# Position-biased softmax on one core: the first chunk in one transfer, a bias table of 16 packets, and a last cut of two rows on eleven and nine DMA engines

## The chip, the cores and the metric

The kernel runs on one core of one Trainium2 chip. The metric is device microseconds for one execution. Before the change the median of three runs is 1329.23 us (1328.12 to 1330.56). One more execution was taken under the hardware profiler; all rows of a profile come from that execution.

## The reference

The inputs are `logits` of shape (2, 8, 2112, 2112) and `rel_bias` of shape (8, 33), both float32. The bias depends only on the head and on the distance between row and column, clipped to 16 on either side.

```python
rel = pos[:, None] - pos[None, :]
bias = rel_bias[:, np.clip(rel, -16, 16) + 16]
logits = logits + bias[None, :, :, :]
logits = logits - logits.max(axis=-1, keepdims=True)
exp = np.exp(logits)
return (exp / exp.sum(axis=-1, keepdims=True)).astype(np.float32)
```

So 285.5 MB of logits come in, and as much goes out.

## The kernel before

**Tiling.** The 2 x 8 x 2112 rows of 2112 numbers are dealt out in order: each of the 128 partitions owns 264 consecutive rows (`ROWS`), an eighth of one head. A chunk is six rows (`R`) of every partition, 128 x 12672 numbers, 6336 KB, and there are 44 chunks. Four buffers X0 to X3 hold chunks; a chunk is loaded into its buffer, worked on in place, and stored from there.

**The table.** VectorE first builds a strip M of 2375 numbers per partition in PSUM, from which the bias of any row is a window. For that, L101 loads all 264 numbers of `rel_bias` to each of the 128 partitions (on ScalarE's DMA queue), L135 multiplies by a mask that leaves the partition's own head, L139 adds over the eight heads into `rbS`, and L143 to L159 spread the result into M. The iotas of L105 and L106 on GpSimd tell each partition its head and its eighth.

**The steady loop.** For every four chunks VectorE copies a window of M to F (L164). Per chunk it then does six fused passes that add the bias, negate, and take the minimum, which is minus the row's maximum (L170); ScalarE does six exponentials with a sum (L179); VectorE takes three reciprocals at a time (L187) and scales the rows (L191).

**The DMA queue.** All loads and stores of logits are issued by SyncE (SP), in the order of the program. First stand the loads of chunk 0, as six transfers of one row per partition (L92; the first five count up the semaphore `pre`, the sixth counts up `ld[0]`), and the loads of chunks 1 to 3 (L82). VectorE waits for `pre` ahead of its loop (L194). In SP's loop (L208) a store waits until its rows are scaled (L85), and the load of chunk n + 4 waits until the store of chunk n has landed (L211), as they share a buffer.

**The end.** The last chunk is stored in four transfers: rows 0 to 2 of it on 128 partitions (L215), and then the list `TAIL` (L217): the rest up to column `CUT` of the chunk's 12672 on 128 partitions, then the columns from `CUT` on, for partitions 0 to 109, and the same columns for partitions 110 to 127. Here `CUT` is 12672 - 768, so the last two transfers hold 768 numbers (3072 bytes) of each partition. The list is laid out for a split of each transfer over the core's 16 DMA engines by partitions: eight partitions to each engine out of 128, ten to each of eleven engines out of 110 (`MOST` is written as 11 * 10), and two to each of nine engines out of 18. SP's final waits (L226, L227) end the program.

Of the kernel before, what the change touches and what calls it, by code (L numbers as in the profile page):

```python
# [15 lines left out]
def kernel(  # L16
# [6 lines left out]
    nc = tc.nc  # L23
    P = 128
    B, H, S, S2 = logits.shape
    assert S == S2
    MR = 16
    W = 2 * MR + 1
    ROWS = B * H * S // P
    PB = S // ROWS  # L30
    assert ROWS * P == B * H * S and PB * ROWS == S and PB == H == 8
    R = 6
    NBUF = 4
# [4 lines left out]
    MW = S + ROWS - 1  # L38
    FW = S + STEP - 1
    BIG = 3.0e38  # L40
    CUT = R * S - 768
    MOST = 11 * 10
    TAIL = [(0, P, HALF * S, CUT), (0, MOST, CUT, R * S), (MOST, P, CUT, R * S)]

    io = ctx.enter_context(tc.tile_pool(name="io", bufs=1))
    X = [io.tile([P, R * S], FP32, tag=f"X{b}", name=f"X{b}") for b in range(NBUF)]
    F = io.tile([P, FW], FP32, tag="F", name="F")
    rbS = io.tile([P, W], FP32, tag="rbS", name="rbS")
# [3 lines left out]
    ip = io.tile([P, 3, PB], I32, tag="ip", name="ip")  # L52
# [3 lines left out]
    def view(t, offset, dims):  # L56

        return bass.AP(tensor=t.tensor, offset=t.offset + offset, ap=[[list(t.ap[0])[0], P]] + dims)

    def rows(t, j, n):  # L60

        return bass.AP(tensor=t.tensor, offset=t.offset + j * S, ap=[[ROWS * S, P], [1, n * S]])

    with tc.tile_critical(no_gpsimd_drain=True):
        ld = [nc.alloc_semaphore(f"ld{b}") for b in range(NBUF)]
# [3 lines left out]
        scaled = nc.alloc_semaphore("scaled")  # L69
        inv = nc.alloc_semaphore("inv")  # L70
        rb = nc.alloc_semaphore("rb")
        pre = nc.alloc_semaphore("pre")
        idx = nc.alloc_semaphore("idx")
        dve = nc.alloc_semaphore("dve")
        landed = tc.alloc_semaphore("landed")

        def take(eng, sem, n):
            eng.wait_ge(sem, n).then_inc(sem, -n)  # L78


        def load(j, b):
            nc.sync.dma_start(out=X[b][:, :], in_=rows(logits, j, R)).then_inc(ld[b], 16)  # L82
# [5 lines left out]
            ).then_inc(sem or st[b], 16)  # L88


        for r in range(R):
            nc.sync.dma_start(  # L92
                out=X[0][:, r * S : (r + 1) * S], in_=rows(logits, r, 1)
            ).then_inc(ld[0] if r == R - 1 else pre, 16)
        for n in range(1, NBUF):
            load(n * R, n)

        rbB = view(F, 0, [[1, H * W]])  # L100
        nc.scalar.dma_start(  # L101
            out=rbB,
            in_=bass.AP(tensor=rel_bias.tensor, offset=rel_bias.offset, ap=[[0, P], [1, H * W]]),
        ).then_inc(rb, 16)
        nc.gpsimd.iota(ip[:, 0], pattern=[[0, PB]], base=0, channel_multiplier=1).then_inc(idx, 1)  # L105
        nc.gpsimd.iota(ip[:, 2], pattern=[[1, PB]], base=0, channel_multiplier=0).then_inc(idx, 1)  # L106

        v = nc.vector
        done = [0]

        def then(ins):
            done[0] += 1
            ins.then_inc(dve, 1)

        def settle():
            v.wait_ge(dve, done[0])

        SC = H * W
        mask = [F[:, SC + i * PB : SC + (i + 1) * PB] for i in range(9)]
        dp, dh, eq, hm, gt, le, lt, ra, rz = mask  # L120
        v.wait_ge(idx, 2)
        then(v.tensor_scalar(out=ip[:, 1], in0=ip[:, 0], scalar1=3, scalar2=7,  # L122
                             op0=ALU.logical_shift_right, op1=ALU.bitwise_and))
# [7 lines left out]
        for m, op in ((eq, ALU.is_equal), (gt, ALU.is_gt), (le, ALU.is_le), (lt, ALU.is_lt)):  # L131
# [4 lines left out]
            out=view(F, 0, [[W, H], [1, W]]), in0=view(F, 0, [[W, H], [1, W]]),  # L136
            in1=view(F, SC + 3 * PB, [[1, H], [0, W]]), op=ALU.mult))
        settle()
        then(v.tensor_reduce(out=rbS[:, :], in_=view(F, 0, [[1, W], [W, H]]),  # L139
                             axis=mybir.AxisListType.X, op=ALU.add))  # L140
        settle()
        low, high = rbS[:, W - 1 : W], rbS[:, 0:1]
        then(v.tensor_scalar(out=ra, in0=gt, scalar1=low, scalar2=None, op0=ALU.mult))  # L143
        then(v.tensor_scalar(out=rz, in0=gt, scalar1=low, scalar2=None, op0=ALU.mult))  # L144
        then(v.tensor_tensor(  # L145
            out=view(F, 0, [[W, PB], [1, W]]), in0=view(F, SC + 2 * PB, [[1, PB], [0, W]]),
            in1=view(rbS, W - 1, [[0, PB], [-1, W]]), op=ALU.mult))
# [6 lines left out]
            out=view(M, U, [[ROWS, PB], [1, W]]), in0=view(F, 0, [[W, PB], [1, W]]),  # L154
            in1=view(F, SC + 8 * PB, [[1, PB], [0, W]]), op=ALU.add))
        then(v.tensor_copy(out=view(M, U + W, [[ROWS, PB], [1, ROWS - W]]),  # L156
                           in_=view(F, SC + 7 * PB, [[1, PB], [0, ROWS - W]])))
        then(v.tensor_copy(out=M[:, 0:U], in_=low.to_broadcast([P, U])))  # L158
# [32 lines left out]
                    v.tensor_scalar_mul(out=x, in0=x, scalar1=rec[:, r : r + 1]).then_inc(scaled, 1)  # L191

        v.sem_inc(dve, -done[0])
        take(v, pre, 16 * (R - 1))  # L194
        with nc.Fori(0, ROWS - STEP + 1, STEP, engines=[ENG.DVE]) as j:  # L195
            strip(j)
            take(v, dve, 1)
# [19 lines left out]
        for p0, p1, c0, c1 in TAIL:  # L217
            nc.sync.dma_start(
                out=bass.AP(
                    tensor=out.tensor, offset=out.offset + (p0 * ROWS + (N - 1) * R) * S + c0,  # L220
                    ap=[[ROWS * S, p1 - p0], [1, c1 - c0]],
                ),
                in_=X[(N - 1) % NBUF][p0:p1, c0:c1],
# [34 lines left out]
```

## Time and profile before

| what | value |
|---|---|
| median of three runs | 1329.23 us |
| the profiled execution | 1328.04 us |
| its span, first to last instruction | 1326.3 us |
| VectorE busy | 976.7 us (74%) |
| ScalarE busy | 576.0 us (43%) |
| moved by DMA | 571.11 MB in 13830 packets |

The span is 1.7 us shorter than the execution's own time, and that execution is 1.2 us below the median. A row of the instruction list names line, engine, operation and tiles, then busy time and mean duration, then the idle time ahead. In a table by stretches, "DMA share" is the mean busy share of the 16 DMA engines; a packet is counted whole in the stretch in which it starts, so a share can exceed 1. In the list of DMA packets of a stretch, the packets under 512 bytes are the semaphore updates, and the line that begins with GB/s cuts the stretch into 40 equal slices and gives the bytes of packets that start in each.

### The profile page before, as it was taken

The page shows a single profiled execution, that of the slowest core. Times are in us where ns is not written, and L with a number is a line of the kernel's source. Part 1 is how long each engine was busy: PE and PEld are TensorE (multiplying, and loading weights), DVE is VectorE, ACT ScalarE, POOL GpSimd, SP SyncE. Part 2 cuts the span into 40 slices and gives each one's busy share as a digit, 9 for nine tenths or more (in the row PEclk, how much of TensorE's full clock was granted, in tenths as well). Part 3 has the DMA queues.
Part 4 walks back from the last instruction along what each step waited for, and adds up shares of the span by engine and source line. Part 5 has one row for each costly group of instructions (what it writes and reads, how often), then busy time and mean ns, then how long its engine had stood idle before and what let it go on. Part 6 is the DMA issues. An engine that isn't in the chain of part 4 may idle for free. (4 is left out here: it accounts for less than half of the span.)

```text
span 1326.3 us, 2458 instructions
## 1 busy us (share of the span) xinstructions
DVE 976.7 (74%) x911; ACT 576.0 (43%) x539; POOL 0.4 (0%) x6
## 2 busy tenths in 40 slices
DVE  5999667777877776687778777677877786677772
ACT  2565333444444343345445333434444443334441
POOL 0000000000000000000000000000000000000000
DMA  9999999999999999999999999999999999999998
GB/s 386 436 428 436 433 430 434 430 433 430 437 434 430 433 434 434 436 428 437 434 433 430 437 437 431 431 437 436 433 430 437 431 430 439 434 434 430 437 433 375
DMA packets 13830, 571.11 MB, mean 431 GB/s; under 512 B 1540, under 2 KB 1668, under 8 KB 1796
## 3 DMA queue, kind: packets, MB, share of 16 engines
q1 hardware_dynamic: 13684, 570.96, 99.6%
q10 hardware_dynamic: 144, 0.14, 0.1%
q14 instruction: 2, 0.02, 0.0%
HBM read 285.61 MB, written 285.47 MB: 431 GB/s over the span
## 5 line engine op out<-in xcount | busy, mean ns | idle before, releaser
L170 DVE CUSTOM_DVE_ANT_0 X<-X,F 128x2112 f32<-128x2112 f32 x264 | 605.2, 2355 | 300.1 <-DVEq L78 300.1
L179 ACT ACTIVATE X<-X,nmax 128x2112 f32<-128x2112 f32 x264 | 542.3, 2054 | 538.3 <-ACTq L78 517.1
L191 DVE TENSOR_SCALAR X<-X,rec 128x2112 f32<-128x2112 f32 x264 | 332.5, 1316 | 13.2
L179 ACT ACT_TABLE_LOAD x11 | 14.1, 1283 | 183.2 <-ACTq L78 183.2
L179 ACT ACTIVATION_READ_ACCUMULATOR X<-X,nmax 128x1 f32 x264 | 49.7, 188 | 0.0
L164 DVE COPY F<-M 128x2135 f32 x11 | 26.1, 2375 | 7.2 <-DVEq L78 7.2
L170 DVE DVE_READ_ACCUMULATOR2_ANT nmax<- 128x1 f32 x264 | 22.0, 83 | 0.0
L187 DVE RECIPROCAL rec<-tot 128x3 f32<-128x3 f32 x88 | 15.0, 171 | 0.0
L135 DVE TENSOR_TENSOR F<-F 128x264 f32<-128x264 f32 x1 | 0.4, 434 | 4.6 <-DMA F<-in_rel_bias_dram 4.6
L156 DVE COPY M<-F 128x1848 f32<-128x1848 f32 x1 | 2.1, 2077 | 0.0
L122 DVE TENSOR_SCALAR ip<-ip 128x8 int32<-128x8 int32 x1 | 0.2, 172 | 1.3 <-POOL ip L106 1.3
L139 DVE TENSOR_REDUCE rbS<-F 128x33 f32<-128x264 f32 x1 | 0.6, 609 | 0.0
L153 DVE TENSOR_TENSOR M<-F 128x264 f32<-128x264 f32 x1 | 0.4, 441 | 0.0
L145 DVE TENSOR_TENSOR F<-F,rbS 128x264 f32<-128x264 f32 x1 | 0.4, 427 | 0.0
L132 DVE TENSOR_SCALAR F<-F 128x8 f32<-128x8 f32 x4 | 0.4, 166 | 0.0
L158 DVE COPY M<-rbS 128x247 f32<-128x247 f32 x1 | 0.4, 406 | 0.0
L143 DVE TENSOR_SCALAR F<-F,rbS 128x8 f32<-128x8 f32 x1 | 0.2, 231 | 0.0
L149 DVE SCALAR_TENSOR_TENSOR F<-F,rbS 128x8 f32<-128x8 f32 x1 | 0.2, 227 | 0.0
L144 DVE TENSOR_SCALAR F<-F,rbS 128x8 f32<-128x8 f32 x1 | 0.2, 225 | 0.0
L150 DVE SCALAR_TENSOR_TENSOR F<-F,rbS 128x8 f32<-128x8 f32 x1 | 0.2, 222 | 0.0
L128 DVE TENSOR_TENSOR F<-ip 128x8 f32<-128x8 int32 x1 | 0.2, 167 | 0.0
L125 DVE TENSOR_TENSOR F<-ip 128x8 f32<-128x8 int32 x1 | 0.2, 166 | 0.0
(9 smaller groups left out, 1.2 us busy)
## 6 DMA issues: line engine op xcount, KB each, us to landing
X<-in_logits_dram SPq DMA_DIRECT2D x43, 6336.0 KB, 44.6
out_dram<-X SPq DMA_DIRECT2D x43, 6336.0 KB, 52.6
X<-in_logits_dram SPq DMA_DIRECT2D x6, 1056.0 KB, 12.8
out_dram<-X SPq DMA_DIRECT2D x1, 3168.0 KB
out_dram<-X SPq DMA_DIRECT2D x1, 2784.0 KB
out_dram<-X SPq DMA_DIRECT2D x1, 330.0 KB
F<-in_rel_bias_dram ACTq DMA_DIRECT2D x1, 132.0 KB, 6.1
out_dram<-X SPq DMA_DIRECT2D x1, 54.0 KB
```

Source lines behind the costliest of these rows:

```text
L132: then(v.tensor_scalar(out=m, in0=dp, scalar1=0.0, scalar2=None, op0=op))
L135: then(v.tensor_tensor(out=view(F, 0, [[W, H], [1, W]]), in0=view(F, 0, [[W, H], [1, W]]), in1=view(F, SC + 3 * PB, [[1, H], [0, W]]), op= ...
L139: then(v.tensor_reduce(out=rbS[:, :], in_=view(F, 0, [[1, W], [W, H]]), axis=mybir.AxisListType.X, op=ALU.add))
L145: then(v.tensor_tensor(out=view(F, 0, [[W, PB], [1, W]]), in0=view(F, SC + 2 * PB, [[1, PB], [0, W]]), in1=view(rbS, W - 1, [[0, PB], [-1, ...
L153: then(v.tensor_tensor(out=view(M, U, [[ROWS, PB], [1, W]]), in0=view(F, 0, [[W, PB], [1, W]]), in1=view(F, SC + 8 * PB, [[1, PB], [0, W]] ...
L156: then(v.tensor_copy(out=view(M, U + W, [[ROWS, PB], [1, ROWS - W]]), in_=view(F, SC + 7 * PB, [[1, PB], [0, ROWS - W]])))
L158: then(v.tensor_copy(out=M[:, 0:U], in_=low.to_broadcast([P, U])))
L164: v.tensor_copy(out=F[:, :], in_=M[:, bass.ds(ROWS - STEP - j, FW)]).then_inc(dve, 1)
L170: v.tensor_tensor_reduce(out=x, in0=x, in1=F[:, STEP - 1 - r : STEP - 1 - r + S], scale=-1.0, scalar=BIG, op0=ALU.add, op1=ALU.min, accum_ ...
L179: nc.scalar.activation(out=x, in_=x, func=EXP, scale=-1.0, bias=nmax[:, r : r + 1], accum_out=tot[:, r : r + 1],).then_inc(expd, 1)
L187: v.reciprocal(out=rec[:, r0 : r0 + HALF], in_=tot[:, r0 : r0 + HALF]).then_inc(inv, 1)
L191: v.tensor_scalar_mul(out=x, in0=x, scalar1=rec[:, r : r + 1]).then_inc(scaled, 1)
```

## The change

It has three parts. The six row transfers of chunk 0 become one 6336 KB transfer, and the semaphore `pre` and the wait for it go. The bias table is loaded to 16 partitions only, every eighth, ahead of the loads in the program's text; VectorE first clears that part of F, and ScalarE's queue waits for that. Two 32 x 32 transposes with a copy between them, and a copy behind, then spread the reduced table over each group of eight partitions. Last, `CUT` becomes 12672 - 4224, so that the last two transfers hold the last two rows (16896 bytes of each partition), and the first one of `TAIL` holds one row.

```diff
-    CUT = R * S - 768
+    CUT = R * S - 2 * S
     MOST = 11 * 10
     TAIL = [(0, P, HALF * S, CUT), (0, MOST, CUT, R * S), (MOST, P, CUT, R * S)]
...
-        for r in range(R):
-            nc.sync.dma_start(
-                out=X[0][:, r * S : (r + 1) * S], in_=rows(logits, r, 1)
-            ).then_inc(ld[0] if r == R - 1 else pre, 16)
-        for n in range(1, NBUF):
-            load(n * R, n)
-        rbB = view(F, 0, [[1, H * W]])
-        nc.scalar.dma_start(
-            out=rbB,
-            in_=bass.AP(tensor=rel_bias.tensor, offset=rel_bias.offset, ap=[[0, P], [1, H * W]]),
-        ).then_inc(rb, 16)
...
+        then(v.memset(F[:, 0 : H * W], 0.0))
+
+        nc.scalar.wait_ge(dve, 1)
+        nc.scalar.dma_start(
+            out=bass.AP(tensor=F.tensor, offset=F.offset, ap=[[PB * list(F.ap[0])[0], P // PB], [1, H * W]]),
+            in_=bass.AP(
+                tensor=rel_bias.tensor, offset=rel_bias.offset, ap=[[0, P // PB], [1, H * W]]
+            ),
+        ).then_inc(rb, 16)
+        for n in range(NBUF):
+            load(n * R, n)
...
+        Q = 32
+        RB, RT, RC, RW = [SC + 9 * PB + 2 * Q * i for i in range(4)]
+        then(v.memset(F[:, RB : RB + 2 * Q], 0.0))
...
-        then(v.tensor_reduce(out=rbS[:, :], in_=view(F, 0, [[1, W], [W, H]]),
+        then(v.tensor_reduce(out=F[:, RB : RB + W], in_=view(F, 0, [[1, W], [W, H]]),
                              axis=mybir.AxisListType.X, op=ALU.add))
+        settle()
+        then(v.transpose(out=F[:, RT : RT + 2 * Q], in_=F[:, RB : RB + 2 * Q]))
+        settle()
+        then(v.tensor_copy(out=view(F, RC, [[Q, 2], [PB, Q // PB], [1, PB]]),
+                           in_=view(F, RT, [[Q, 2], [PB, Q // PB], [0, PB]])))
+        settle()
+        then(v.transpose(out=F[:, RW : RW + 2 * Q], in_=F[:, RC : RC + 2 * Q]))
+        settle()
+        then(v.tensor_copy(out=rbS[:, :], in_=F[:, RW : RW + W]))
...
-        take(v, pre, 16 * (R - 1))
```

More of the change, by code (lines that the diff above doesn't have):

```diff
@@ L71 @@
         rb = nc.alloc_semaphore("rb")
-        pre = nc.alloc_semaphore("pre")
         idx = nc.alloc_semaphore("idx")
@@ L88, in store @@
             ).then_inc(sem or st[b], 16)
-        for r in range(R):
-            nc.sync.dma_start(
-                out=X[0][:, r * S : (r + 1) * S], in_=rows(logits, r, 1)
-            ).then_inc(ld[0] if r == R - 1 else pre, 16)
-        for n in range(1, NBUF):
-            load(n * R, n)
-        rbB = view(F, 0, [[1, H * W]])
-        nc.scalar.dma_start(
-            out=rbB,
-            in_=bass.AP(tensor=rel_bias.tensor, offset=rel_bias.offset, ap=[[0, P], [1, H * W]]),
-        ).then_inc(rb, 16)
-        nc.gpsimd.iota(ip[:, 0], pattern=[[0, PB]], base=0, channel_multiplier=1).then_inc(idx, 1)
-        nc.gpsimd.iota(ip[:, 2], pattern=[[1, PB]], base=0, channel_multiplier=0).then_inc(idx, 1)
         v = nc.vector
@@ L116, in settle @@
             v.wait_ge(dve, done[0])
+        then(v.memset(F[:, 0 : H * W], 0.0))
[8 more added lines that the diff above has]
+            load(n * R, n)
+        nc.gpsimd.iota(ip[:, 0], pattern=[[0, PB]], base=0, channel_multiplier=1).then_inc(idx, 1)
+        nc.gpsimd.iota(ip[:, 2], pattern=[[1, PB]], base=0, channel_multiplier=0).then_inc(idx, 1)
         SC = H * W
```

## The prediction

> **What bounds the kernel now.** I read the page's first three parts, then the table by stretches, then the DMA packets of the last microsecond.
>
> ```profile
> span 1326.3 us, 2458 instructions
> DVE 976.7 (74%) x911; ACT 576.0 (43%) x539; POOL 0.4 (0%) x6
> DMA  9999999999999999999999999999999999999998
> q1 hardware_dynamic: 13684, 570.96, 99.6%
> q10 hardware_dynamic: 144, 0.14, 0.1%
> ```
>
> No compute engine is near full; the 16 DMA engines are, in every slice but the last. SP's queue (q1) fills 99.6% of their span. The chain of waits names almost nothing here, since a transfer is no instruction. So the time is how long the slowest DMA engine needs for its share, from its first byte to its last; a change can save only at the two ends, or through fewer or better packets. The table by stretches shows the two ends and, between them, the steady rate (columns: stretch, its length, DVE, ACT and POOL busy with counts, clock, DMA share, GB/s):
>
> ```profile
> 0.00:2.00 2.00, 0.63 (x5) 0.00 (x0) 0.42 (x6) 1.00 0.00 2
> 2.00:3.00 1.00, 0.43 (x5) 0.00 (x0) 0.00 (x0) 1.00 0.49 86
> 3.00:4.00 1.00, 0.00 (x0) 0.00 (x0) 0.00 (x0) 1.00 0.60 116
> 4.00:5.00 1.00, 0.00 (x0) 0.00 (x0) 0.00 (x0) 1.00 0.77 208
> 5.00:6.00 1.00, 0.00 (x0) 0.00 (x0) 0.00 (x0) 1.00 0.93 343
> 6.00:9.00 3.00, 1.83 (x6) 0.00 (x0) 0.00 (x0) 1.00 1.03 432
> 9.00:19.00 10.00, 3.10 (x6) 0.00 (x0) 0.00 (x0) 1.00 1.01 426
> 100.00:1200.00 1100.00, 813.40 (x747) 479.98 (x451) 0.00 (x0) 1.00 1.00 433
> ...
> 1303.00:1313.00 10.00, 0.28 (x1) 0.00 (x0) 0.00 (x0) 1.00 0.97 419
> ...
> 1320.00:1321.00 1.00, 0.00 (x0) 0.00 (x0) 0.00 (x0) 1.00 1.06 443
> 1321.00:1322.00 1.00, 0.00 (x0) 0.00 (x0) 0.00 (x0) 1.00 0.66 269
> 1322.00:1323.00 1.00, 0.00 (x0) 0.00 (x0) 0.00 (x0) 1.00 0.47 198
> 1323.00:1324.00 1.00, 0.00 (x0) 0.00 (x0) 0.00 (x0) 1.00 0.32 135
> 1324.00:1325.00 1.00, 0.00 (x0) 0.00 (x0) 0.00 (x0) 1.00 0.09 38
> ```
>
> The steady rate is 433 GB/s, or 27.06 GB/s for each engine. By 9.00 us, 2.05 MB had started (4 + 86 + 116 + 208 + 343 + 3 x 432 KB), which at 433 is 4.74 us of work: the engines are as far as if they had begun at full rate at 4.26 us. The last stretches show that engines end at very different times: from 1321 on, 0.66, 0.47, 0.32 and 0.09 of them work. That is room of a few us for whoever spreads the last bytes well, and the `TAIL` list does just that. Who ends last is told by the packets of the last microsecond, 40 slices of 0.025 us:
>
> ```profile
> GB/s 0 0 123 0 0 891 123 0 0 0 0 123 0 0 0 0 123 0 0 0 0 123 0 0 0 0 0 0 0 0 0 0 0 0 0 0 0 0 0 0
> DMA packets 12, 0.04 MB, mean 38 GB/s; under 512 B 6, under 2 KB 6, under 8 KB 11
> ```
>
> A slice of 891 GB/s is one packet of 22272 bytes: an engine that serves only the 128-partition transfer of the tail is at its eighth packet, from about 1324.14. At 27.06 GB/s it lasts 0.82 us and ends at 1324.96. The slices of 123 are packets of 3072 bytes, five in a row every 0.12 us: one engine at its share of the extra columns, whose last begins at about 1324.54 and ends at 1324.65. So the two kinds of engine end within 0.3 us of each other: 768 columns balance them.
>
> **The change part by part.**
>
> *The tail.* Bytes per engine behind the half store, before and after:
> - Nine engines with ten and two packets of the extra transfers: 8 x 22272 + 12 x 3072 = 215040, then 8 x 8448 + 12 x 16896 = 270336. That is 55296 more, 2.04 us at 27.06 GB/s.
> - Two engines with ten packets: 208896, then 236544; 1.02 us more.
> - Five engines with none: 178176, then 67584; 4.09 us less.
>
> So the slowest engine without extra columns moves from 1324.96 to 1320.9 and no longer matters, and the slowest with them moves from 1324.65 to 1326.69 if it is one of the nine, or to 1325.67 if it is one of the two. The end moves by +1.73 or +0.71; nine of the eleven are of the first kind, so I take **+1.7**. That packets of the extra transfers run at full rate though few engines share them is what the row shows: 3072 bytes every 0.12 us. The unseen size 16896 is bounded by that rate, 25.6 GB/s, and the steady one: 12 of them take 7.9 or 7.5 us, so 0.4 us more at worst, which I keep for the range and else take the steady rate, as the size is nearer to the 50688 bytes of the steady packets.
>
> In the shares from 1321 on, 0.66 to 0.09, the late engines should get less, and both versions give five of them less. The Trainium skill speaks against the form, in "DMA: Bandwidth & Descriptors", section "Rules for kernel authors": keep a multiple of 16 as the outermost size, because a count such as 110 leaves engines out. By that rule the two rows would go out on 128 partitions: 8 x 25344 bytes on each engine, 0.91 us more than now for the last one, instead of 1.7. In this trace the rule does not hold for 768 columns, where leaving engines out ends evenly; no run yet shows it for 4224.
>
> The issue of these transfers stays hidden:
>
> ```profile
> 1299.36 0.33 SPq L86 DMA_DIRECT2D out_dram<-X  x1
> 1303.37 2.32 SPq L218 DMA_DIRECT2D out_dram<-X  x3
> ```
>
> SP is done at 1305.69, while the engines are kept busy (0.97 in 1303 to 1313) by the store before and the half store. The first extra packet is wanted some 4 us earlier than now (five 128-partition rows become three plus one), still about ten us behind its issue. If that cover failed, the missing part would be added to the end one for one.
>
> *The first chunk and the table.* Two shares are worked out from rows of the start.
>
> ```profile
> L92 SPq DMA_DIRECT2D X<-in_logits_dram x6: 415/572/968, 1.0 to 4.2; - x6
> DMA to landing us min/median/max: 7.6/12.8/17.3
> F<-in_rel_bias_dram ACTq DMA_DIRECT2D x1, 132.0 KB, 6.1
> 0.92 0.40 ACTq L101 DMA_DIRECT2D F<-in_rel_bias_dram  x1
> 0.97 3.81 SPq L92 DMA_DIRECT2D X<-in_logits_dram  x6
> ```
>
> Packets of one row: 6.49 MB at 426 GB/s are 15.23 us, at 433 14.98: 0.25 us saved. By landings (first row 0.97 + 7.6 = 8.6, sixth 4.2 + 17.3 = 21.5, five rows in 12.9, six in 15.5) it is 0.5. I take 0.35. Bias bytes: 0.135 MB become 0.017 MB; at 433 GB/s that is 0.27 us. Third, the ramp: the table was issued ahead of the loads and its packets came first. From 2.00 to 3.00 only 86 of 433 GB/s moved, a loss of 0.8 us, and
>
> ```profile
> DMA packets 53, 0.09 MB, mean 86 GB/s; under 512 B 0, under 2 KB 49, under 8 KB 49
> ```
>
> 49 of 53 packets were the table's, and four were loads where 16 engines could each have had one. Now SP issues first, with 50688-byte packets that keep an engine busy for 1.87 us each. Lower bound: the ramp stays, 0 (a later start has no reason: SP's first transfer waits for nothing and is as large per engine in descriptors). Upper bound: full rate from 2.00, 4.26 - 2.00 = 2.26 us. I take twelve sixteenths of the 0.8, 0.6 us, as it is nearest to the row. Sum of the start: 0.35 + 0.27 + 0.6 = **-1.2**, ends -0.5 and -3.0.
>
> The added wait stands on ScalarE's queue: behind it are the table's transfer and then exponentials that need chunk 0 anyway. VectorE gets two clears, two transposes and two copies of at most 264 columns:
>
> ```profile
> L135 DVE TENSOR_TENSOR F<-F 128x264 f32<-128x264 f32 x1 | 0.4, 434 | 4.6 <-DMA F<-in_rel_bias_dram 4.6
> L122 DVE TENSOR_SCALAR ip<-ip 128x8 int32<-128x8 int32 x1 | 0.2, 172 | 1.3 <-POOL ip L106 1.3
> 11.97 0.17 DVE L159 COPY M<-rbS 128x16 f32<-128x16 f32 x1
> 19.31 2.38 DVE L164 COPY F<-M 128x2135 f32 x1 [7.17 <-DVEq L78]
> 43.89 22.22 SPq L86 DMA_DIRECT2D out_dram<-X  x2
> ```
>
> Between 172 and 434 ns each, 1.0 to 2.6 us in all, one of them ahead of the table's issue. M was ready at 12.14 and VectorE then idled 7.17 us for `pre`; that covers them, and with `pre` gone the strip's copy can run before chunk 0 lands. I cost this at nothing, and a gain on VectorE at nothing too: the four loads keep the engines busy until 4.3 + 4 x 15 = 64 us, and the first store is issued at 43.89, 20 us ahead of need. If the table came later by more than that, each us would count.
>
> The Trainium skill, same page, section "Queues, rings and completion order", says that an engine takes turns between queues by whole packets; by it each table packet may stand behind one or more 1.87 us packets and land some us later than the 6.1 of now. That too would be eaten by the 7.17 us and the 20 us.
>
> **Sum:** +1.7 - 1.2 = +0.5 us on the profiled execution, 1328.0 to 1328.5. It ran 1.2 us under the median, so the forecast for a median is 1329.23 + 0.5 = **1329.7**.
>
> **Rivals.**
> - *A, forecast*: 1329.7, chance 0.58.
> - *B, the start pays more and the tail less*: ramp at its upper bound and the last extra engine one of the two, 0.71 - 3.0 = -2.3, 1326.9; half way, 1328.3. For it: the ramp loses 2.26 us. Against: some ramp must remain, and nine of eleven engines take twelve packets. Chance 0.2, nearly all of it within 0.2%.
> - *C, slower*: the extra packets, read by eleven engines from ten neighbouring partitions each, get in each other's way once they are long. Place: the last 7.5 us (12 x 16896 bytes at 27.06 GB/s). Each 10% of stretch costs 0.75 us. Against it: 3072-byte packets ran every 0.12 us. To be slower by 0.2% (2.66 us) in all, 2.2 us must be added, a stretch of 29%; at 35%, 1332.3. Chance 0.14.
> - *D, the start also undoes the engines' unevenness*, so that the last of the nine is no longer late: the ends spread over the last 4 us, and an end 2.5 us earlier together with the tail's +1.7 and a start at its upper bound, -3.0, gives -3.8, 1325.4. Against: the spread need not come from the start. Chance 0.04.
> - *E, the change doesn't do what it says*: the last transfers run on 16 engines after all. Then each engine has 8 x 25344 bytes, 24576 more than now on the last one, +0.9 - 1.2, 1328.9. Against: five small packets in a row from one engine. Chance 0.04.
>
> **How the numbers follow.** A measurement of this kernel can tell about 0.2%, 2.7 us. A, E and B lie within it, but for 0.01 of B that I count as faster: same 0.81, faster 0.04 + 0.01 = 0.05, slower 0.14. The range takes A with its bounds (+1.7 - 0.5 = +1.2, 1330.4) and on top the spread of the three runs (1.3 us above their median), to 1331.7, which also holds the 0.4 us of slower packets, and B down to 1327.2. That leaves out most of C, D and the end of B, less than 0.2.
>
> **What would show it.** In the profile after, by stretches: over 200 GB/s from 2 to 3 us right for the ramp, near 86 wrong. The strip's copy (now L173) starts before 17 us, not at 19.31, and the first pass of chunk 0 (now L179) near 20.8 instead of 22.0. In the last 5 us, DMA share at 0.6 and less, with packets of 16896 bytes alone, and the last ending near 1325.5 in its own span. If packets of 16896 bytes start more than 0.65 us apart on one engine, C is at work. The forecast is wrong if the sum of start and tail leaves -2.3 to +1.2, or if the stretch from 100 to 1200 no longer moves 433 GB/s.

## The result, and the profile after

The changed kernel takes 1336.62 us (median of six runs, 1334.97 to 1337.61) against 1329.62 us before (six runs, 1328.12 to 1330.56): 7.0 us more, a ratio of 1.0052 with a 95% interval of 1.0039 to 1.0064. The forecast was +0.5 us, and its range ended at 1331.7. The profiled execution took 1337.1 us, its span 1335.0 us.

The first rows answer to those shown of before: the page's opening, then the table by stretches of the changed kernel (same columns).

```profile
span 1335.0 us, 2458 instructions
DVE 977.8 (73%) x917; ACT 575.2 (43%) x539; POOL 0.4 (0%) x6
q1 hardware_dynamic: 12964, 570.96, 99.2%
q10 hardware_dynamic: 32, 0.02, 0.0%
```

```profile
0.00:2.00 2.00, 0.85 (x7) 0.00 (x0) 0.42 (x6) 1.00 0.08 25
2.00:3.00 1.00, 0.43 (x5) 0.00 (x0) 0.00 (x0) 1.00 2.39 760
3.00:4.00 1.00, 0.00 (x0) 0.00 (x0) 0.00 (x0) 1.00 0.00 0
4.00:5.00 1.00, 0.00 (x0) 0.00 (x0) 0.00 (x0) 1.00 1.76 760
...
100.00:1200.00 1100.00, 805.67 (x739) 471.59 (x442) 0.00 (x0) 1.00 1.00 433
...
1320.00:1324.00 4.00, 0.00 (x0) 0.00 (x0) 0.00 (x0) 1.00 0.74 239
1324.00:1326.00 2.00, 0.00 (x0) 0.00 (x0) 0.00 (x0) 1.00 0.34 101
1326.00:1327.00 1.00, 0.00 (x0) 0.00 (x0) 0.00 (x0) 1.00 0.23 76
...
1330.00:1331.00 1.00, 0.00 (x0) 0.00 (x0) 0.00 (x0) 1.00 0.16 68
1331.00:1332.00 1.00, 0.00 (x0) 0.00 (x0) 0.00 (x0) 1.00 0.13 51
1332.00:1333.00 1.00, 0.00 (x0) 0.00 (x0) 0.00 (x0) 1.00 0.12 51
```

The start is better than forecast: 760 GB/s worth of packets begin from 2 to 3 us, where it was 86, then nothing from 3 to 4, and 760 again from 4 to 5. All 16 engines begin within a us, and their second packets begin together again. (These first packets are slow: 760 at a share of 2.39 is 318 GB/s at a full share.) The steady rate, 433 GB/s, has not changed, and from 0 to 1300 us both kernels moved 432 GB/s. The loss is in the last stretches: from 1324 on, a third of the engines work, from 1330 on two or three of them (0.16 and 0.13 of 16), to 1333.7. VectorE shows the gain at the front:

```profile
15.17 0.17 DVE L168 COPY M<-rbS 128x16 f32<-128x16 f32 x1
15.81 2.38 DVE L173 COPY F<-M 128x2135 f32 x1 [0.47 <-DVEq L202]
18.80 2.36 DVE L179 CUSTOM_DVE_ANT_0 X<-X,F 128x2112 f32<-128x2112 f32 x1 [0.60 <-DVEq L77]
```

Its first pass on chunk 0 starts at 18.80 instead of 22.00, 3.2 us earlier. That is how much sooner the whole of chunk 0 was there; the DMA engines, which set the time, are ahead by less. The first 30 us, before and after:

```profile
0.00:30.00 30.00, 16.37 (x28) 5.51 (x6) 0.42 (x6) 1.00 0.92 376
```

```profile
0.00:30.00 30.00, 20.66 (x36) 8.71 (x8) 0.42 (x6) 1.00 0.96 406
```

30 GB/s more over 30 us are 0.9 MB, which at 433 GB/s is some 2 us of work (an estimate, as packets are counted whole). So some 2 us are gained at the front, and some nine are lost from there to the end. How the engines stand to each other shows in the packets of 4 us early in the kernel, 40 slices of 0.1 us; 507 is one packet of 50688 bytes that starts in that slice. First before, then after, both from 30 to 34 us:

```profile
GB/s 1014 0 507 507 1014 2028 507 507 0 507 0 507 0 0 0 507 507 0 0 1014 0 1014 0 1521 1521 1014 0 0 507 507 0 0 0 0 507 507 0 507 507 507
```

```profile
GB/s 0 0 0 0 0 0 0 0 2534 2534 1014 1014 1014 0 0 0 0 0 0 0 0 0 0 0 0 0 507 3042 1521 1014 1521 507 0 0 0 0 0 0 0 0
```

Before, the 16 engines begin their packets spread over some 1.4 of the 1.87 us that a packet lasts. After, all 16 begin within some 0.5 us, in both rounds of packets shown. The forecast had looked at how much time the start took, not at this order.

### The profile page after: what moved, and what is told of

It is laid out like the page before. It is cut to its first block, busy times and chain, and to the rows that moved or that the text cites. A ratio compares the mean times of both kernels' runs of the same rounds, so it can differ in the third digit from the quotient of the medians.

```text
span 1335.0 us, 2458 instructions
## 1 busy us (share of the span) xinstructions
DVE 977.8 (73%) x917; ACT 575.2 (43%) x539; POOL 0.4 (0%) x6
## 5 line engine op out<-in xcount | busy, mean ns | idle before, releaser
L188 ACT ACT_TABLE_LOAD x11 | 14.1, 1283 | 185.2 <-ACTq L77 185.2
```

Source lines behind the costliest of these rows:

```text
L188: nc.scalar.activation(out=x, in_=x, func=EXP, scale=-1.0, bias=nmax[:, r : r + 1], accum_out=tot[:, r : r + 1],).then_inc(expd, 1)
```

## The experiments

Theory S: the table's 128 packets, ahead of the loads, set the engines apart; without that a few engines fall far behind by the end, and some of these get extra rows from the last cut. Rival T: the long packets of the cut get in each other's way and make the loss. Rival R, later: the spread at the start doesn't matter, and the new way of building the table costs the time. Times are medians of 10 to 12 runs (five in the last experiment) beside 33 to 35 runs of the kernel before on the same chip (nine in the last). The experiments ran on four chips: the first four on one, the next four on a second, the next four on a third, the last on a fourth. Differences in us are those of the medians. The ratio with its interval comes from a comparison of all these runs and is not just the quotient of the two medians. Five experiments add a useless load of table numbers; nothing uses these numbers, but VectorE waits for them to land before it masks the table.

**The cut alone.** The kernel before with

```diff
-    CUT = R * S - 768
+    CUT = R * S - 2 * S
```

> The kernel before, with the last cut of two rows alone. Theory S (the new start makes a few DMA engines fall some 6 to 11 us behind the others, and these are engines that get extra rows; the cut itself costs what was forecast): +1.7 to +2.1 us over the kernel before, about 1331.5. Theory T (the long extra packets get in each other's way and make nearly all of the loss): +7 to +9 us, about 1338. In its profile S expects the DMA share to fall to zero near 1327 of the span, T near 1333.

Measured: 1332.70 against 1330.12 us, ratio 1.0019 (1.0009 to 1.0028), +2.6 us. T is out: the cut is not the bulk of the loss. The cost is more than the 1.7 forecast, which still lies within the interval of 1.2 to 3.7 us, and the stretches of the profile suggest a reason:

```profile
1318.00:1322.00 4.00, 0.00 (x0) 0.00 (x0) 0.00 (x0) 1.00 0.84 338
1322.00:1324.00 2.00, 0.00 (x0) 0.00 (x0) 0.00 (x0) 1.00 0.63 228
```

At the end of the kernel before, a full share would move 167 / 0.40 = 418 GB/s (1322 to 1324 in a table by two us, shown below). Here it is 338 / 0.84 = 402 in the first stretch and 228 / 0.63 = 362 in the second, and in the changed kernel 239 / 0.74 = 323 (1320 to 1324, above): packets there last 1.1, 1.2 and 1.3 times as long as at the steady 433. So packets are slower at the end with the long cut, at the place that rival C named, and 2.6 - 1.7 = 0.9 us is the room for it. That the long packets hinder each other is inferred; no run changed their size alone.

**The start alone.** The changed kernel with the old cut:

```diff
-    CUT = R * S - 2 * S
+    CUT = R * S - 768
```

> The changed kernel with the last cut at 768 columns again, so the new start alone. Theory S: +4.5 to +6 us over the kernel before, about 1335, with two to four DMA engines alone at work in the last 8 us. Theory T: the start is a gain, -1.2 to -2.5 us, about 1328.

Measured: 1332.81 against 1330.12 us, ratio 1.0019 (1.0008 to 1.0029), +2.7 us. S was right in sign and too high in size. The end of its profile, in stretches of two us, first before and then the start alone:

```profile
1318.00:1320.00 2.00, 0.00 (x0) 0.00 (x0) 0.00 (x0) 1.00 0.86 368
1320.00:1322.00 2.00, 0.00 (x0) 0.00 (x0) 0.00 (x0) 1.00 0.86 356
1322.00:1324.00 2.00, 0.00 (x0) 0.00 (x0) 0.00 (x0) 1.00 0.40 167
1324.00:1326.00 2.00, 0.00 (x0) 0.00 (x0) 0.00 (x0) 1.00 0.05 19
```

```profile
1318.00:1320.00 2.00, 0.00 (x0) 0.00 (x0) 0.00 (x0) 1.00 0.78 325
1320.00:1322.00 2.00, 0.00 (x0) 0.00 (x0) 0.00 (x0) 1.00 0.38 160
1322.00:1324.00 2.00, 0.00 (x0) 0.00 (x0) 0.00 (x0) 1.00 0.31 134
1324.00:1326.00 2.00, 0.00 (x0) 0.00 (x0) 0.00 (x0) 1.00 0.27 109
1326.00:1328.00 2.00, 0.00 (x0) 0.00 (x0) 0.00 (x0) 1.00 0.13 40
1328.00:1330.00 2.00, 0.00 (x0) 0.00 (x0) 0.00 (x0) 1.00 0.03 11
```

Before, the engines come to an end one after the other until 1325. With the new start most are done early, and 0.31 of 16, five engines, work on alone. Which five is told by the packets that start from 1324 on in the start alone:

```profile
DMA packets 57, 0.33 MB, mean 44 GB/s; under 512 B 11, under 2 KB 11, under 8 KB 47
```

47 - 11 = 36 of them are the small packets of the extra transfers, three times twelve. So, most simply, three of the five late engines are among the nine that carry twelve extra packets. That is where the two parts of the change meet: with 768 columns the twelve packets cost 1.5 us, with two rows 7.5 us (12 x 16896 bytes at the steady rate).

**One transfer, old table.** The kernel before with

```diff
...
-        for r in range(R):
-            nc.sync.dma_start(
-                out=X[0][:, r * S : (r + 1) * S], in_=rows(logits, r, 1)
-            ).then_inc(ld[0] if r == R - 1 else pre, 16)
-        for n in range(1, NBUF):
+        for n in range(NBUF):
             load(n * R, n)
...
-        take(v, pre, 16 * (R - 1))
```

> The kernel before with chunk 0 in one transfer, and the table still read by all 128 partitions. Theory S, if it is the table's 128 packets ahead of the loads that set the engines apart: no loss, -0.3 to -0.6 us. Theory S, if it is the six small transfers that did it: +4 to +6 us. Theory T: -0.3 to -0.6 us.

Measured: 1329.50 against 1330.12 us, ratio 1.0000 (0.9989 to 1.0011). The single transfer shows no loss. Eight of its twelve runs lie from 1328.58 to 1329.80, four from 1331.32 to 1334.26.

**Small table, six row transfers.** The kernel before with the changed kernel's 16-packet table (issued after the clear) and its spreading on chip, nothing else.

> The kernel before with the table of 16 packets, spread on chip, and chunk 0 still in six row transfers. Theory S, if the table's packets set the engines apart: +4 to +6 us. Theory S, if the six transfers did: -0.3 to -1 us. Theory T: -0.3 to -1 us.

Measured: 1334.50 against 1330.12 us, ratio 1.0030 (1.0021 to 1.0039), +4.4 us; every one of ten runs at 1333.46 or more. So the new table does it, by its 16 packets, by its late issue, or by its spreading on chip. Its end, in the same stretches:

```profile
1318.00:1320.00 2.00, 0.00 (x0) 0.00 (x0) 0.00 (x0) 1.00 0.69 277
1320.00:1322.00 2.00, 0.00 (x0) 0.00 (x0) 0.00 (x0) 1.00 0.32 135
1322.00:1324.00 2.00, 0.00 (x0) 0.00 (x0) 0.00 (x0) 1.00 0.34 145
1324.00:1326.00 2.00, 0.00 (x0) 0.00 (x0) 0.00 (x0) 1.00 0.28 117
```

Eleven engines have ended soon after 1320 and five work on, for some six us and more. Its packets from 1324 on again hold 36 small ones:

```profile
DMA packets 61, 0.42 MB, mean 56 GB/s; under 512 B 11, under 2 KB 11, under 8 KB 47
```

**The old table, issued late.** The kernel before with the table's issue moved behind a clear on VectorE:

```diff
...
+        then(v.memset(F[:, 0 : H * W], 0.0))
+        nc.scalar.wait_ge(dve, 1)
         rbB = view(F, 0, [[1, H * W]])
         nc.scalar.dma_start(
...
```

> The kernel before, its table still of 128 packets, but issued only after a clear on VectorE, so behind the first loads as in the changed kernel. Theory S1 (what counts is that the table's packets stand ahead of the loads and let the engines begin one after the other): like the small table alone, +3 to +4.5 us, with five late engines at the end. Theory S2 (what counts is the number of the table's packets, wherever they stand): within 1 us of before. Theory R (the spread at the start has nothing to do with it, the on-chip spreading of the table costs time): within 1 us of before.

Measured: 1334.54 against 1329.89 us, ratio 1.0027 (1.0018 to 1.0036), +4.7 us (by the ratio 3.6, 2.4 to 4.8). In its profile the share from 1322 to 1326 is 0.31 and 0.29, again five late engines, as S1 expected. This kernel has all 128 packets and no spreading on chip, and loses as much as the small table. R falls, and S2 with it: what counts is that the 128 packets stand ahead of the loads.

**The new start, and a useless table ahead of it on ScalarE's queue.** The start alone, and

```diff
...
+        nc.scalar.dma_start(
+            out=view(F, 1000, [[1, H * W]]),
+            in_=bass.AP(tensor=rel_bias.tensor, offset=rel_bias.offset, ap=[[0, P], [1, H * W]]),
+        ).then_inc(dum, 16)
         nc.scalar.wait_ge(dve, 1)
...
```

> The new start with 768 columns at the end, and besides a load of 128 table packets to unused columns, issued ahead of all loads, that nothing needs. Theory S1: the engines begin apart again, and the time returns to within 1 us of before, though there is more to do. Theory S2: the same. Theory R: no better than the new start alone, +2.5 us or more.

Measured: twelve runs in two groups, five from 1329.04 to 1329.77 and seven from 1333.16 to 1334.81 (median 1333.29 against 1329.89; ratio 1.0010, 0.9998 to 1.0022). Neither theory had said that. The profiled run is one of the second group (1334.81 us), and suggests why: issued 0.03 us ahead of SP's first load, the useless table still landed 14.1 us later, where the table before took 6.1.

```profile
0.93 0.41 ACTq L103 DMA_DIRECT2D F<-in_rel_bias_dram  x1
0.96 2.02 SPq L81 DMA_DIRECT2D X<-in_logits_dram  x4
```

```profile
F<-in_rel_bias_dram ACTq DMA_DIRECT2D x1, 132.0 KB, 14.1
```

In this run ten packets of the loads began from 2 to 3 us (565 GB/s), where before there were four (86 GB/s), so most engines had a long packet ahead of the rest of the table, though the table's first packets still came first. That points to a race at the start. It would also explain the runs of the single transfer and of the kernel before that lie near 1334 us (one of 33 at 1334.78); no profile of such a run was taken, nor one of the first group here, so that is inferred.

**The changed kernel with a plain end**, the last three rows in one transfer of 128 partitions:

```diff
-    TAIL = [(0, P, HALF * S, CUT), (0, MOST, CUT, R * S), (MOST, P, CUT, R * S)]
+    TAIL = [(0, P, HALF * S, R * S)]
```

> The changed kernel with the last three rows in one transfer on 128 partitions. If three of the five late engines get extra rows, as the landings of the new start alone suggest, the extra columns cost there what they save before: 1330.5 to 1333, at or a little under the new start with 768 columns (+2.5 us). If the late engines were the five without extra rows, as before: 0.5 to 1 us over the new start with 768 columns, 1333.5 to 1334.

Measured: 1331.89 against 1329.89 us, ratio 1.0010 (1.0001 to 1.0018). With the new start 768 extra columns bring nothing over none (the intervals of the two overlap), and two rows of them cost some 4 to 5 us more than this plain end (+5.6 and +7.0 against +2.0 us, on different chips). The plain end with the old start was not run.

**The table twice ahead** (the useless table load on ScalarE's queue added to the kernel before).

> The kernel before with the 128-packet table load issued twice, both ahead of the loads. Theory S: the engines begin further apart, and the latest at the end is no further behind than before; the extra bytes cost 0.3 us and the start 0.5 to 1 us: -1 to +1 us. Theory R: +0.5 to +1 us.

Measured: 1330.59 against 1329.89 us, ratio 1.0005 (0.9996 to 1.0014); it settles nothing.

**The table first, on SP's own queue**, with the single transfer, so that no race between two queues can change the order:

```diff
...
-        nc.scalar.dma_start(
+        nc.sync.dma_start(
             out=rbB,
             in_=bass.AP(tensor=rel_bias.tensor, offset=rel_bias.offset, ap=[[0, P], [1, H * W]]),
         ).then_inc(rb, 16)
+        for n in range(NBUF):
+            load(n * R, n)
...
```

> The kernel before with chunk 0 in one transfer and the 128-packet table issued by SP itself, ahead of its loads, so that it cannot lose the race of 0.05 us against the first load. Theory S (packets of the table ahead of the loads let the engines begin 1.5 to 2 us apart, and then the late ones at the end are fewer us behind): all runs near 1328.5 to 1330, none of the 1332 to 1334 that the kernel before has now and then; -0.5 to -1.5 us, with the table's landing early and the loads' landings spread by 1.5 to 2 us. Theory R (the runs near 1334 have another cause): the same share of such runs as before, and 0 to -0.5 us.

Measured: 1329.23 against 1329.81 us, ratio 0.9995 (0.9986 to 1.0004), all eleven runs from 1327.95 to 1330.88. No run lies above 1331, as S says, while the kernel before had seven of 33 above it. At that share eleven runs without one would come about by chance about once in 14 times ((26/33) to the power of 11), so this supports S without settling it. That the median is better is not clear of the noise; no version of the study is shown to be faster than the kernel before.

**Sixteen packets first.** The late table, and ahead of the loads on SP a useless load of one table packet for each engine.

> The kernel before with the table issued late, and a load of 16 table packets, one for each engine, on SP ahead of the loads, that nothing needs. Theory S: one packet each does not set the engines apart, so it stays like the late table, +3 to +4.5 us. If being ahead is enough, whatever the number: within 1 us of before.

Measured: 1332.57 against 1329.81 us, ratio 1.0019 (1.0010 to 1.0028), +2.8 us, no run under 1331.31. Being ahead is not enough: 16 packets do not do what 128 do. The loss is somewhat less than expected. The profile fits the idea of the spread only in part. Its loads begin almost as slowly as before (100, 131 and 297 GB/s from 2 to 5 us, before 86, 116 and 208), and from 30 to 34 us its engines begin spread over some 1.4 us, as before, though with nine of them within 0.3 us:

```profile
GB/s 0 0 507 0 0 0 0 507 0 507 0 1521 2028 1014 0 507 507 507 507 0 0 507 0 0 0 0 507 507 0 0 2028 2028 507 0 1014 507 507 0 0 507
```

Still five engines are late at its end (0.34 and 0.31 of 16 from 1322 to 1326). So the width of the spread early in the kernel does not by itself tell the end.

**The changed kernel, with 128 useless table packets first on SP.**

> The changed kernel, cut of two rows and all, with a load of 128 table packets on SP ahead of the loads, that nothing needs. Theory S: the start's loss goes and the cut's stays, +1.7 to +3 us over the kernel before, where the changed kernel has +7. Theory R: +7 us or more.

Measured: 1332.63 against 1329.81 us, ratio 1.0022 (1.0013 to 1.0031), +2.8 us. The changed kernel lost 7.0 us in the result and 5.6 in the repeat below, which ran on another chip than this; so half of its loss or more goes away by adding a load whose numbers nothing needs. What stays is as much as the cut alone cost, +2.6.

**Two tables first on SP.**

> As the table first on SP, but with two such loads of 128 packets. If more packets ahead spread the engines further and that helps at the end: -1 to 0 us against the table first. If the spread is made by one load already, it costs 0.3 to 1 us more than the table first.

Measured: 1330.98 against 1329.81 us, ratio 1.0006 (0.9997 to 1.0015): by the medians 1.8 us worse than one table first, though the two intervals overlap. A second load shows no gain. Two of its eleven runs lie at 1332.46 and 1333.26, so the claim of theory S, that a table first on SP's own queue rules out such runs, does not hold here.

**The changed kernel again**, on the fourth chip; the expectation's two terms of 2.5 us come from the first chip.

> The changed kernel as it is, on the chip of these experiments. If the two losses simply add: 2.5 (new start) + 2.5 (cut) = +5 us. If they reinforce each other, because three of the late engines of the new start are among the nine that get twelve extra packets: +6.5 to +8 us, as the result shows.

Measured: 1336.04 against 1330.40 us, ratio 1.0044 (1.0031 to 1.0058), +5.6 us. The sum of the parts, 5, and the +7 of the result both lie in its interval of 4.1 to 7.7 us. Whether the two losses reinforce each other, or only add, stays open.

## Why the prediction was wrong, point by point

- *What bounds the kernel*: right. Engines busy in every slice, 433 GB/s in the middle in both profiles, VectorE's additions (a first pass 3.2 us earlier all the same) and the issue of the last transfers hidden. The table landed 7.8 us after its issue instead of 6.1, and M was ready at 15.34 instead of 12.14; that was still over 3 us ahead of the first pass at 18.80.
- *The start, -1.2 us*: this is the step that failed. The start alone measured +2.7 us. As a gain at the front the term was even too small: the engines were some 2 us of work ahead by 30 us. But the forecast took this sum for the time to the end, as if each engine kept its place to the others from there on; it counted the slow ramp as loss alone and put the price of losing the table's packets ahead of the loads at nothing. The late table (+4.7), the small table (+4.4) and the changed kernel with a useless table first (+2.8, where the changed kernel itself has +5.6 and +7.0) show that the 128 packets ahead of the loads are worth several us. Without them, in the profiles of the start alone, the small table and the late table, eleven engines end by about 1321 us and five work on for five us and more.
- *Rival D*, that the start changes the engines' unevenness, had the right place and the wrong sign; I gave it 0.04 and only as a gain. I wrote that the spread "need not come from the start" and left it there.
- *The tail, +1.7 us*: right in mechanism, +2.6 measured (interval 1.2 to 3.7, which holds the forecast). The term that looks mis-sized is the packet of 16896 bytes, which I took at the steady rate; the stretches gave 1.1 to 1.2 times as long in the cut alone and 1.3 times in the changed kernel. That is rival C in part: in the cut alone it stays short of the 29% from which C was to decide, and the last packets of the changed kernel run at full rate again (68 / 0.16 = 425 GB/s from 1330 on).
- *What I could have seen*: the shares of 0.66, 0.47, 0.32 and 0.09 at the end of before were read as a fixed property of the engines that the cut had only to match. They depend on how the run of 1300 us begins, and the change touched that beginning.
- The Trainium skill, "DMA: Bandwidth & Descriptors", section "Rules for kernel authors", says to coalesce many small transfers into one large one. The single transfer for chunk 0, one of 6336 KB for six of 1056 KB, is such a step; alone it showed neither gain nor loss (ratio 1.0000, 0.9989 to 1.0011).

What remains open is the mechanism between start and end: why engines that begin within 0.5 us of each other lose five of their number by 5 us and more, while engines that begin over some 1.4 us end one after the other within a few us. The runs show cause and effect, not the link. That it is the spread of the engines, and not something else about the 128 packets, is inferred: no run spread the engines in another way, and the sixteen packets fit it only in part. Nor does the order of the start simply last. From 600 to 604 us, first before and then after, ten engines begin within 0.5 us of each other before, and eleven within 0.6 us after, where five have fallen out of step:

```profile
GB/s 0 0 0 0 1014 0 507 507 3041 0 0 0 507 507 0 0 507 1014 507 0 0 0 507 507 0 1014 507 2535 0 0 0 1014 0 0 507 507 1014 0 0 0
```

```profile
GB/s 0 1014 0 2534 1014 0 1014 0 0 507 0 0 507 0 0 507 0 0 1014 507 507 1521 1014 1014 507 507 0 0 507 0 0 507 0 507 0 0 0 1014 507 507
```

A shared resource that each packet meets at the same moment is a guess. That the late engines are the same in every run was not shown either.

## What to carry to other kernels

In a kernel bound by its DMA engines, what stands ahead of the first loads can change how the engines end 1300 us later: test a change of the first transfers by the end of the profile, not by how soon the first chunk lands. An uneven last store that was fitted to which engines are late has to be fitted again when the beginning changes; giving the same engines more was the wrong way to go here. Where two queues issue within 0.05 us of each other at the start and the order matters, one queue for both is worth a try; here it was not shown to be faster.

## What the hardware showed that I had not expected

Besides the above: in the changed kernel, the first change from loads to stores costs time in itself. The changed kernel around it, then the kernel before around its own:

```profile
60.00:61.00 1.00, 1.00 (x2) 0.00 (x0) 0.00 (x0) 1.00 1.80 507
61.00:62.00 1.00, 1.00 (x2) 0.00 (x0) 0.00 (x0) 1.00 1.09 304
62.00:63.00 1.00, 1.00 (x2) 0.00 (x0) 0.00 (x0) 1.00 0.00 0
```

```profile
62.00:63.00 1.00, 1.00 (x2) 0.00 (x0) 0.00 (x0) 1.00 1.29 558
63.00:64.00 1.00, 1.00 (x2) 0.00 (x0) 0.00 (x0) 1.00 0.70 304
```

After, 507 + 304 = 811 KB take 1.80 + 1.09 = 2.89 us of all engines, where 433 GB/s would take 1.87: 1.0 us lost on each engine. Before, 862 KB take 1.99, as they should. So about half of the lead of some 2 us was gone by 62 us. That engines in step always pay this is not shown: the late table, whose engines also begin together early on, moved 406 GB/s at a share of 0.94 from 60 to 66 us, the steady rate. And an issue 0.03 us ahead on another queue did not settle the time: with the same kernel, the new start with a useless table on ScalarE's queue, runs fell into two groups 4 us apart.
